# The last output tile of a hybrid encoder layer, computed in two runs of tokens

## The chip, the cores and the metric

The kernel runs on one core of a Trainium2 chip. A core has five engines with instruction queues of their own: TensorE (PE; PEld in a profile is its weight load), VectorE (DVE), ScalarE (ACT), GpSimd (POOL) and SyncE (SP, which only issues transfers here), beside 16 DMA engines. The metric is the device time of one execution in microseconds (us); less is better. The profile is of one execution, whose own time is given beside its span, the time from its first to its last instruction.

## The reference

One layer of a streaming encoder works on 256 prompt tokens and 32 sample tokens together, 288 in all, with a model width of 2048. A pooling mixer and a state-space mixer come first, then a gated feed-forward part, and each half ends with a normalised residual. Only the end matters here:

```python
up = hn @ p['w_up']
up, new_fconv = causal_dwconv(up, hist_fconv, p['ffn_conv_w'], p['ffn_conv_b'])
gate, val = up[..., :D_FF], up[..., D_FF:]
f = (jax.nn.silu(gate) * val) @ p['w_down']
x = x + rmsnorm(f, p['norm_ffn_post'])
```

`rmsnorm` divides each token's row of 2048 by the root of its mean square. So no output of a token is known before all 2048 columns of its `f` are: each of the 16 output tiles of `w_down` adds to the sum of squares. Everything is float32.

## The kernel before

**Layout.** Activations lie turned: 128 features in the partitions, 288 tokens along the free axis (`NT`). `BLK` names the three blocks of tokens: tokens 0 to 127 (first block), 128 to 255 (second block) and the 32 samples. A float32 product is made of three products in the type fp32r: weights and activations are each split into a high part (`hi`, made by ScalarE) and a low part (`lo`, the rest, made by VectorE). `mm3` (L162) issues them: high by high, high by low, low by high. Each of the three lines loads a 128x128 weight and streams 288 columns.

**`project`** (L167) fetches weights on SP's queue (`fetch_w`), splits them (`split_w`) and runs `mm3` over K tiles, for two output tiles of 128 features at a time. Hooks let other work be placed at a K group, and `done` is called with each finished accumulator. Accumulators come from a PSUM pool of five banks (`acc_ps`), other PSUM tiles from a pool of three (`aux_ps`).

**The down projection** runs in two halves of K, 22 tiles each. The first half's results lie in SBUF as `part`. The second half runs over `f2`, the last 22 activation tiles, in the loop at L1083: eight projections of two output tiles each. For each tile `down_out` (L1071) adds the accumulator to `part[t]`, squares it, and scales it by `g_ffn_post`. For tiles 0 to 13 the squares are summed over tiles in `fsum` on GpSimd; for tiles 14 and 15 `feature_sums` (L1059) sums them over features on TensorE, straight into `p_f`. That is a product with a column of ones: two over 128 tokens each and four over the 32 samples, whose result is wanted in four groups of partitions. `fsum` is summed the same way once, ahead of the last group of K tiles.

**Back to tokens.** The output has tokens in rows. Tiles 0 to 13 are turned through DRAM: VectorE transposes 32x32 blocks (`blocks_out`, L203), SP writes them to `fd` and reads them back as `ft` (a tile of 128 tokens by 512 features for each quarter q and block b; the fourth quarter's is `ft3`, 256 features wide) and `ft_s` for the samples. Tiles 14 and 15 are turned by TensorE into the PSUM tiles `last` (`to_tokens`, L1036). `xr` and `xr_s` hold the residual in the same layout.

**The end.** `token_rstd` (L588 on) makes the three columns of factors `rf` from `p_f` with one square root and one reciprocal. Then `y_out` (L1100) multiplies `ft` by the factor and adds it to `xr` on VectorE, and SP sends the result out, 256 KB at a time: three quarters of both blocks, then the samples (sent from ScalarE's queue, L1115), then the last quarter, in two instructions for each block because its halves lie in `ft3` and in `last`.

A scheduler places instructions in each engine's queue by priorities; `keep_in_program_order` pins an instruction to its place in the text. In the built program the last projection alternates its two output tiles after every K group, and the sums and turns of tiles 14 and 15 follow the last product.

Of the kernel before, what the change touches and what calls it, by code (L numbers as in the profile page):

```python
# [8 lines left out]
F32 = mybir.dt.float32  # L9
F32R = mybir.dt.float32r  # L10
AF = mybir.ActivationFunctionType
ALU = mybir.AluOpType
# [4 lines left out]
P = 128  # L17
TC = {"schedule_with_timeline_sim": True}
D_MODEL = 2048
NP_ = 256  # L20
NS = 32
NT = NP_ + NS
# [6 lines left out]
KD = D_MODEL // P  # L29
# [4 lines left out]
BLK = ((0, P), (P, P), (NP_, NS))  # L34
WINDOWS = (2, 4, 8, 16)
HALF = NF // 2
# [9 lines left out]
def body(  # L46
# [38 lines left out]
    act, dve, pool, pe, sp = nc.scalar, nc.vector, nc.gpsimd, nc.tensor, nc.sync  # L85
# [10 lines left out]
    const = ctx.enter_context(tc.tile_pool(name="const", bufs=1))  # L96
# [3 lines left out]
    acc_ps = ctx.enter_context(tc.tile_pool(name="acc_ps", bufs=5, space=PSUM))  # L100
# [3 lines left out]
    def aux(shape, name):  # L104
        return aux_ps.tile(shape, F32, tag="aux", name=name)
# [22 lines left out]
    def fetch_w(view, kb, nk, c0, nc_):  # L128
        raw = wpool.tile([P, nk, nc_], F32, tag="raw", name="raw")
        with tc.high_priority(offset=ahead[0]):  # L130
            sp.dma_start(out=raw, in_=view[:, kb : kb + nk, c0 : c0 + nc_])
        return raw

    def split_w(raw, kb, nk, nc_, after=()):

        out = []
        step = min(nk, 1024 // nc_)
        for k in range(0, nk, step):
            n = min(step, nk - k)
# [22 lines left out]
    def mm3(out, wh, wl, a, start, stop):  # L162
        pe.matmul(out, wh, a[:, 0, :], start=start, stop=False)  # L163
        pe.matmul(out, wh, a[:, 1, :], start=False, stop=False)  # L164
        pe.matmul(out, wl, a[:, 0, :], start=False, stop=stop)  # L165
# [82 lines left out]
    start = ExitStack()  # L248
# [20 lines left out]
    for i, v in enumerate((ssd_dt_bias, ssd_a_log, ssd_d)):  # L269
# [5 lines left out]
        out=pf_in[:, 4:6, :], in_=state_ffn_conv.rearrange("o b r (t p) -> t (o b r) p", p=P)  # L275
# [77 lines left out]
    p_ = aux([P, NT], "prs")  # L353
# [7 lines left out]
    pb, pah, g_mix_post, g_ffn_pre, g_ffn_post, pa, p_scale, g_ssd, pc, pf = prm  # L361
# [76 lines left out]
    r = htile("r", tag="z")  # L438
# [21 lines left out]
    for b, (o, go) in enumerate(((0, 0), (P, 256), (TAIL, MW - P))):  # L460
        p_ = aux([P, 3, HEADS], "ptok")
# [11 lines left out]
    p_ = aux([P, 2 * NX], "phv")  # L473
# [6 lines left out]
    for i in range(4):  # L480
        o = btile("bc")
# [5 lines left out]
    for gi in range(2):  # L487
        blocks_out(b_d, gi, bc[gi], mp)
        p_ = aux([P, MW], "pcb")
# [98 lines left out]
    def token_rstd(p_, scale, name):  # L588

        o = const.tile([P, 3], F32, tag="trs", bufs=2, name=name)  # L590
        act.activation(o, p_[:, 0:3], AF.Sqrt, bias=eps_t, scale=scale)
        dve.reciprocal(o, o)
        return o
# [228 lines left out]
    for gi in range(2):  # L822
        c = slice(gi * P, (gi + 1) * P)
# [76 lines left out]
    for s in range(KD + 2):  # L900
# [98 lines left out]
    part = []  # L999
# [34 lines left out]
    last = {}  # L1034

    def to_tokens(t):  # L1036

        if t < KD - 2:
            blocks_out(fd, t, part[t], fp)
            q, n = t // 4, (t % 4 + 1) * P  # L1040
            if t % 4 == 3 or t == KD - 3:
                c = slice(512 * q, 512 * q + n)
                for b in range(2):
                    sp.dma_start(out=ft[2 * q + b][:, :n], in_=fd[b * P : (b + 1) * P, c])
                sp.dma_start(out=ft_s[NS * q : NS * (q + 1), :n], in_=fd[NP_:NT, c])
            return
        j = t - KD + 2
        if j == 0:
            last.update({b: aux([P, 2 * P], "pft") if b == 2 else acc_ps.tile([P, 2 * P], F32, tag="acc", name="pft") for b in range(3)})
        for b, (o, n) in enumerate(BLK):  # L1050
            c = slice(j * P, (j + 1) * P)
            if b == 2:
                pe.matmul(last[b][P - NS :, c], part[t][:, o : o + n], ident, start=True, stop=True)
            else:
                pe.transpose(last[b][:, c], part[t][:, o : o + n], ident)
        if j == 1:
            act.activation(ft_s[P - NS :, 2 * P :], last[2][P - NS :, :], AF.Copy)

    def feature_sums(sq, first_, last_):  # L1059
        for b in range(2):  # L1060
            pe.matmul(
                p_f[:, b : b + 1], sq[:, b * P : (b + 1) * P], ones[:, 0:1],
                start=first_ and b == 0, stop=False, skip_group_check=True,
            )
        for q in range(4):
            pe.matmul(
                p_f[NS * q : NS * q + NS, 2:3], sq[:, NP_:], ones[:, 0:1],
                start=False, stop=last_ and q == 3, skip_group_check=True,
            )

    def down_out(t, p_):  # L1071
        dve.tensor_tensor(part[t], part[t], p_, op=ALU.add)
        if t < KD - 2:
            sq_add(fsum, part[t], fp, t == 0)
        else:
            q = fp.tile([P, NT], F32, tag="fr", bufs=2, name="fsq")
            with tc.high_priority(offset=400):
                act.activation(q, part[t], AF.Square)
            feature_sums(q, False, t == KD - 1)
        act.activation(part[t], part[t], AF.Copy, scale=g_ffn_post[:, t : t + 1])  # L1080

    n_tok = [0]
    for m in range(0, KD, 2):  # L1083
        def hook(kb, n):
            if m and kb == 16:
                while n_tok[0] < m:
                    to_tokens(n_tok[0])
                    n_tok[0] += 1
            if m == KD - 2 and kb == 16:
                feature_sums(fsum, True, False)  # L1090

        project(
            wdv[:, HALF:, :], [(m * P, 256)], f2, [(0, 8), (8, 8), (16, 6)], hook,
            lambda j, p_: down_out(m + j, p_),
        )
    to_tokens(KD - 2)
    to_tokens(KD - 1)
    rf = token_rstd(p_f, 1.0 / D_MODEL, "rf")

    def y_out(q, b):  # L1100

        x = xr[2 * q + b]
        f_ = ft[2 * q + b]
        for o, n, src in (
            ((0, 512, f_),) if q < 3 else ((0, 2 * P, f_[:, : 2 * P]), (2 * P, 2 * P, last[b]))
        ):
            c = slice(o, o + n)
            dve.scalar_tensor_tensor(x[:, c], src, rf[:, b : b + 1], x[:, c], op0=ALU.mult, op1=ALU.add)  # L1108
        sp.dma_start(out=y_prompt[0][b * P : (b + 1) * P, 512 * q : 512 * (q + 1)], in_=x)

    for q in range(3):
        y_out(q, 0)
        y_out(q, 1)
    dve.scalar_tensor_tensor(xr_s, ft_s, rf[:, 2:3], xr_s, op0=ALU.mult, op1=ALU.add)
    act.dma_start(out=y_sample[0].rearrange("s (q c) -> q s c", q=4), in_=xr_s)  # L1115
    y_out(3, 0)
    y_out(3, 1)
    ffn.close()


# [29 lines left out]
```

## Time and profile before

| | us |
|---|---|
| median of 3 runs | 1357.07 (1357.01 to 1357.39) |
| profiled execution | 1357.63 |
| its span | 1355.8 |
| PE busy | 1337.4 |
| DVE, ACT, POOL busy | 884.0, 667.0, 237.6 |
| granted TensorE clock, mean | 0.996 |

An engine's time is the sum over its instructions, in which overlapping ones count once. A row of the timeline gives start, duration, engine, line, operation and tile (result, then sources), shapes, and how often it stands there in a row. With "x4" the duration is from the first one's start to the last one's end. In brackets stands how long the engine had been idle and what ended that. A product of plain float32 data shows as two records of PE, one of fp32r data as one. The part of the trace that matters is the last 36 us: the projection of tiles 14 and 15 from about 1321, and what comes behind it.

### The profile page before, as it was taken

How to read it: one execution, taken by the hardware profiler on the slowest of the kernel's cores; microseconds unless marked ns; L12 is line 12 of the kernel's file. 1: busy time of each engine (PE TensorE's matmuls, PEld its weight loads, DVE VectorE, ACT ScalarE, POOL GpSimd, SP SyncE). 2: the span in 40 equal slices, each digit the busy share in tenths (PEclk: the TensorE clock that was granted, in tenths of full speed). 3: DMA queues.
4: the chain of work that ended last, by engine and by line, in shares of the span. 5: the costliest groups of instructions: out<-in, count | busy, mean ns of one | idle time of the engine just before them, and what ended most of it. 6: DMA issues, size and time to landing. Idle time of an engine off the chain costs nothing.

```text
span 1355.8 us, 25731 instructions
## 1 busy us (share of the span) xinstructions
PE 1337.4 (99%) x10201; PEld 1327.3 (98%) x10201; DVE 884.0 (65%) x1515; ACT 667.0 (49%) x997; POOL 237.6 (18%) x394
## 2 busy tenths in 40 slices
PE   8999999999999999999999999999999999999996
PEld 7999999999999999999999999999999999999995
DVE  6898988779644469977666643435666667654443
ACT  6557757446534455644444433334444444454441
POOL 3132112222224310311121100001112112101110
PEclk9999999999999999999999999999999999999998
DMA  8879885565756536866545555555545545576652
GB/s 268 249 190 277 257 245 172 156 220 153 241 180 209 170 111 202 244 180 193 171 158 173 160 155 159 169 179 163 179 156 165 177 156 167 168 226 201 189 163 88
DMA packets 300136, 252.13 MB, mean 186 GB/s; under 512 B 75729, under 2 KB 293051, under 8 KB 299887
## 3 DMA queue, kind: packets, MB, share of 16 engines
q1 hardware_dynamic: 296810, 243.20, 59.2%
q0 software_dynamic: 2320, 4.65, 1.2%
q10 hardware_dynamic: 884, 2.63, 0.5%
q8 instruction: 80, 1.31, 0.4%
q14 instruction: 42, 0.34, 0.1%
HBM read 236.13 MB, written 14.31 MB: 185 GB/s over the span
## 4 chain that ended last, share of the span: by engine, by line
PE 98%; DVE 0%; DMA 0%; SPq 0%; issue 0%; DVEq 0%; ACT 0%
PE acc L163 31%; PE acc L165 31%; PE acc L164 31%; PE pst L852 1%; PE py L562 1%; DMA xt<-in_x_prompt 0%; DVE xr L1108 0%; PE acc_x L164 0%; PE acc_x L165 0%; PE acc_x L163 0%; PE py L564 0%; PE pt L301 0%; PE acc L186 0%; PE pt L299 0%; PE acc L185 0%; PE py L568 0%
## 5 line engine op out<-in xcount | busy, mean ns | idle before, releaser
L147 DVE TENSOR_TENSOR wlo<-raw,whi 128x1024 fp32r<-128x1024 f32 (+1 forms) x416 | 493.8, 1189 | 350.7 <-ACT whi L146 340.2
L146 ACT ACTIVATE whi<-raw 128x1024 fp32r<-128x1024 f32 (+1 forms) x416 | 427.0, 1028 | 505.6 <-PE acc L164 429.5
L163 PE MATMUL acc<-hn,whi 128*128 128x288 f32 x1376 | 404.6, 295 | 0.0
L164 PE MATMUL acc<-hn,whi 128*128 128x288 f32 x1376 | 403.5, 294 | 0.0
L165 PE MATMUL acc<-hn,wlo 128*128 128x288 f32 x1376 | 403.2, 294 | 0.0
L164 PEld LDWEIGHTS acc<-hn,whi 128*128 128x128 f32 x1376 | 259.8, 189 | 0.1
L165 PEld LDWEIGHTS acc<-hn,wlo 128*128 128x128 f32 x1376 | 259.6, 189 | 0.0
L163 PEld LDWEIGHTS acc<-hn,whi 128*128 128x128 f32 x1376 | 257.3, 187 | 0.1
L163 PE MATMUL acc<-xn,whi 128*128 128x288 f32 x704 | 209.5, 299 | 0.0
L163 PE MATMUL acc<-fa,whi 128*128 128x288 f32 x704 | 208.6, 296 | 0.0
L164 PE MATMUL acc<-fa,whi 128*128 128x288 f32 x704 | 208.4, 296 | 0.0
L164 PE MATMUL acc<-xn,whi 128*128 128x288 f32 x704 | 208.2, 297 | 0.0
L165 PE MATMUL acc<-fa,wlo 128*128 128x288 f32 x704 | 208.0, 295 | 0.0
L165 PE MATMUL acc<-xn,wlo 128*128 128x288 f32 x704 | 207.5, 297 | 0.0
L164 PEld LDWEIGHTS acc<-xn,whi 128*128 128x128 f32 x704 | 133.8, 190 | 0.3
L165 PEld LDWEIGHTS acc<-xn,wlo 128*128 128x128 f32 x704 | 133.2, 190 | 0.3
L163 PEld LDWEIGHTS acc<-xn,whi 128*128 128x128 f32 x704 | 132.6, 189 | 0.5
L164 PEld LDWEIGHTS acc<-fa,whi 128*128 128x128 f32 x704 | 132.7, 188 | 0.0
L163 PEld LDWEIGHTS acc<-fa,whi 128*128 128x128 f32 x704 | 132.2, 188 | 0.0
L165 PEld LDWEIGHTS acc<-fa,wlo 128*128 128x128 f32 x704 | 132.0, 188 | 0.0
L944 POOL COPY fc_stage<-ebuf 128x4 f32<-128x4 f32 x88 | 27.9, 317 | 505.7 <-DVE ebuf L943 505.7
L950 DVE SCALAR_TENSOR_TENSOR fc<-ebuf,pf,fc 128x290 f32<-128x290 f32 x176 | 90.3, 517 | 2.8 <-ACT fc L948 0.2
(310 smaller groups left out, 1621.6 us busy)
## 6 DMA issues: line engine op xcount, KB each, us to landing
raw<-in_w_up SPq DMA_DIRECT2D x80, 1024.0 KB, 5.2
raw<-in_w_in SPq DMA_DIRECT2D x40, 1024.0 KB, 6.1
raw<-in_w_down SPq DMA_DIRECT2D x32, 1024.0 KB, 5.4
raw<-in_w_out SPq DMA_DIRECT2D x24, 1024.0 KB, 5.9
raw<-in_w_down SPq DMA_DIRECT2D x16, 768.0 KB, 4.6
raw<-in_w_up SPq DMA_DIRECT2D x14, 512.0 KB, 4.2
gb<-g_d SPq DMA_DIRECT2D x8, 832.0 KB, 5.0
raw<-in_w_in SPq DMA_DIRECT2D x6, 512.0 KB, 6.5
```

Of the source, the lines that this page charges most:

```text
L146: act.activation(hi, raw[:, k : k + n, :], AF.Copy)
L147: dve.tensor_tensor(lo, raw[:, k : k + n, :], hi.bitcast(F32), op=ALU.subtract)
L163: pe.matmul(out, wh, a[:, 0, :], start=start, stop=False)
L164: pe.matmul(out, wh, a[:, 1, :], start=False, stop=False)
L165: pe.matmul(out, wl, a[:, 0, :], start=False, stop=stop)
L562: ins = pe.matmul(y[c, 0:256], xw[:, 0, f_], m[:, h, 0:256], start=True, stop=False)
L852: ins = pe.matmul(st[:, o, :], x_, btok[:, gi, b, :], start=b != 1, stop=b != 0)
L944: pool.tensor_copy(fc_stage[:, :, :, i], e[:, 256:324].rearrange("p (s c) -> p s c", c=34)[:, :, 0:2])
L950: dve.scalar_tensor_tensor(c, e[:, r_ : r_ + 290], pf[:, r_, i : i + 1], c, op0=ALU.mult, op1=ALU.add)
```

## The change

- The loop over projections stops after tile 13. The weights of tiles 14 (`A`) and 15 (`B`) are still fetched together, but split one tile at a time, and tile 14 is computed alone, with `mm3` over all 288 tokens. Tiles 12 and 13 are sent to `fd` within it.
- Tile 15 is computed in two runs over its 22 K tiles: first the second block and the samples (`C1`, 160 tokens), then the first block (`C0`, 128 tokens). In `last_mm`, the high and low part of the activations are one moving operand for the high weights (two segments of columns, 320 or 256 in all), whose results lie side by side in one bank; the low weights' product (160 or 128 columns) goes to the first of them. The two are added on VectorE (`add_to`).
- The last K tile has three separate products into a small bank of its own (`p_c`), which is added as the third.
- The sums of `fsum`, now with tile 14's squares added to it, and the turn of tile 14 stand inside run 1. The sums for the second block and samples, their factors, and the turns of tile 15's second block and samples stand inside run 2, and so do these tokens' outputs, except the last quarter. The samples leave on SP's queue.
- `last` has 512 columns: ScalarE copies `ft3` into its first 256, so that the last quarter is one instruction for each block.
- Of the first block's four outputs, the first is made on TensorE: the identity times `xr[0]`, plus a diagonal of the factors (made on ScalarE) times `ft[0]`; ScalarE copies the sum to SBUF. The others stay on VectorE.
- Nearly all of this is pinned to program order.

```diff
-    def feature_sums(sq, first_, last_):
...
+    def first_sums(sq, first_):
+
+        pin(pe.matmul(p_f[:, 0:1], sq[:, :P], ones[:, 0:1], start=first_, stop=not first_, skip_group_check=True))
+
+    def other_sums(sq, first_):
+
+        pin(pe.matmul(p_f[:, 1:2], sq[:, P:NP_], ones[:, 0:1], start=False, stop=False, skip_group_check=True))
         for q in range(4):
-            pe.matmul(
+            pin(pe.matmul(
                 p_f[NS * q : NS * q + NS, 2:3], sq[:, NP_:], ones[:, 0:1],
...
+    def factors(c, name):
+        o = const.tile([P, 3], F32, tag="trs", bufs=2, name=name)[:, c]
+        pin(act.activation(o, p_f[:, c], AF.Sqrt, bias=eps_t, scale=1.0 / D_MODEL))
+        pin(dve.reciprocal(o, o))
+        return o
...
-    for m in range(0, KD, 2):
+    for m in range(0, KD - 2, 2):
...
-    to_tokens(KD - 2)
-    to_tokens(KD - 1)
-    rf = token_rstd(p_f, 1.0 / D_MODEL, "rf")
...
+    A, B = KD - 2, KD - 1
+    K22 = [(0, 8), (8, 8), (16, 6)]
+    raws = [fetch_w(wdv[:, HALF:, :], kb, n, A * P, 256) for kb, n in K22]
+
+    def one_tile(t):
+        out = []
+        for (kb, n), raw in zip(K22, raws):
+            out += split_w(raw[:, :, (t - A) * P : (t - A + 1) * P], kb, n, P)[0]
+        return out
+
+    p_a = acc_ps.tile([P, NT], F32, tag="acc", name="acc")
+    for k, hi, lo in one_tile(A):
+        if k == 8:
+            to_tokens(KD - 4)
+            to_tokens(KD - 3)
+        mm3(p_a, hi, lo, f2[k], k == 0, k == HALF - 1)
+    wb = one_tile(B)
+
+    last = [acc_ps.tile([P, 4 * P], F32, tag="acc", name="pft") for b in range(2)] + [aux([P, 2 * P], "pft")]
+
+    p_b = [acc_ps.tile([P, 2, n], F32, tag="acc", name="acc") for n in (NT - P, P)]
+    p_c = [aux([P, NT - P], "acc_c"), aux([P, P], "acc_c")]
+
+    def tile_out(t, c, p_, sq):
+        with tc.high_priority(offset=400):
+            dve.tensor_tensor(part[t][:, c], part[t][:, c], p_, op=ALU.add)
+            act.activation(sq[:, c], part[t][:, c], AF.Square)
+            act.activation(part[t][:, c], part[t][:, c], AF.Copy, scale=g_ffn_post[:, t : t + 1])
...
+    def last_mm(r, k, hi, lo, c):
+
+        if k == HALF - 1:
+            for i, (w, x) in enumerate(((hi, 0), (hi, 1), (lo, 0))):
+                pin(pe.matmul(p_c[r], w, f2[k][:, x, c], start=not i, stop=i == 2))
+            return
+        o, end = p_b[r], k == HALF - 2
+        pin(pe.matmul(o, hi, f2[k][:, :, c], start=k == 0, stop=end, skip_group_check=True))
+        pin(pe.matmul(o[:, 0, :], lo, f2[k][:, 0, c], start=False, stop=end, skip_group_check=True))
+
+    def add_to(t, c, p_):
+        return pin(dve.tensor_tensor(part[t][:, c], part[t][:, c], p_, op=ALU.add))
...
+    for k, hi, lo in wb:
+        last_mm(0, k, hi, lo, C1)
+        if k == 8:
+            first_sums(fsum, True)
+            other_sums(fsum, True)
+            for b in range(3):
+                turn(A, b)
+            for b in range(2):
+                act.activation(last[b][:, : 2 * P], ft[6 + b][:, : 2 * P], AF.Copy)
+    for x in range(2):
+        add_to(B, C1, p_b[0][:, x, :])
+    tile_out(B, C1, p_c[0], sq[B])
+    for k, hi, lo in wb:
+        last_mm(1, k, hi, lo, C0)
+        if k == 5:
+            other_sums(sq[B], False)
+            rf = factors(slice(1, 3), "rf1")
+        if k == 8:
+            turn(B, 1)
+            turn(B, 2)
+            act.activation(ft_s[P - NS :, 2 * P :], last[2][P - NS :, :], AF.Copy)
...
+    for q in range(3):
+        y_out(q, 1, rf[:, 0:1])
+    pin(dve.scalar_tensor_tensor(xr_s, ft_s, rf[:, 1:2], xr_s, op0=ALU.mult, op1=ALU.add))
+    pin(sp.dma_start(out=y_sample[0].rearrange("s (q c) -> q s c", q=4), in_=xr_s))
+    for x in range(2):
+        add_to(B, C0, p_b[1][:, x, :])
+    add_to(B, C0, p_c[1])
+    pin(act.activation(sq[B][:, C0], part[B][:, C0], AF.Square))
+    y_out(3, 1, rf[:, 0:1])
+    first_sums(sq[B], False)
+
+    p_y = acc_ps.tile([P, 512], F32, tag="acc", name="py_")
+    pin(pe.matmul(p_y, ident, xr[0], start=True, stop=False))
+    rf = factors(slice(0, 1), "rf0")
+    pin(act.activation(part[B][:, C0], part[B][:, C0], AF.Copy, scale=g_ffn_post[:, B : B + 1]))
+    turn(B, 0)
+    diag = fp.tile([P, P], F32, tag="fc", bufs=6, name="diag")
+    pin(act.activation(diag, ident, AF.Copy, scale=rf[:, 0:1]))
+    pin(pe.matmul(p_y, diag, ft[0], start=False, stop=True))
+    pin(act.activation(xr[0], p_y, AF.Copy))
+    y_out(1, 0, rf[:, 0:1])
+    y_out(2, 0, rf[:, 0:1])
+    pin(sp.dma_start(out=y_prompt[0][0:P, 0:512], in_=xr[0]))
+    y_out(3, 0, rf[:, 0:1])
```

Here L1127 and L1128 are the two products of `last_mm` in the changed kernel, L1124 its three products for the last K tile, and `turn` moves one block of a tile into `last` on TensorE.

More of the change, by code (lines that the diff above doesn't have):

```diff
@@ L1033, in body @@
     fd = dram.tile([NT, D_MODEL], F32, name="fd")
-    last = {}
+    pin = tc.keep_in_program_order
     def to_tokens(t):
[L1038 to L1057, printed above, removed]
@@ L1059, in feature_sums @@
-    def feature_sums(sq, first_, last_):
[L1060 to L1064, printed above, removed]
+        blocks_out(fd, t, part[t], fp)
+        q, n = t // 4, (t % 4 + 1) * P
+        if t % 4 == 3 or t == KD - 3:
+            c = slice(512 * q, 512 * q + n)
+            for b in range(2):
+                sp.dma_start(out=ft[2 * q + b][:, :n], in_=fd[b * P : (b + 1) * P, c])
+            sp.dma_start(out=ft_s[NS * q : NS * (q + 1), :n], in_=fd[NP_:NT, c])
@@ L1065, in feature_sums @@
+    def first_sums(sq, first_):
+        pin(pe.matmul(p_f[:, 0:1], sq[:, :P], ones[:, 0:1], start=first_, stop=not first_, skip_group_check=True))
+    def other_sums(sq, first_):
+        pin(pe.matmul(p_f[:, 1:2], sq[:, P:NP_], ones[:, 0:1], start=False, stop=False, skip_group_check=True))
         for q in range(4):
-            pe.matmul(
+            pin(pe.matmul(
                 p_f[NS * q : NS * q + NS, 2:3], sq[:, NP_:], ones[:, 0:1],
-                start=False, stop=last_ and q == 3, skip_group_check=True,
-            )
+                start=False, stop=not first_ and q == 3, skip_group_check=True,
+            ))
@@ L1071, in down_out @@
+    def factors(c, name):
[3 more added lines that the diff above has]
+        return o
     def down_out(t, p_):
         dve.tensor_tensor(part[t], part[t], p_, op=ALU.add)
[L1073 to L1079, printed above, removed]
+        sq_add(fsum, part[t], fp, t == 0)
@@ L1088, in hook @@
                     n_tok[0] += 1
-            if m == KD - 2 and kb == 16:
-                feature_sums(fsum, True, False)
         project(
@@ L1095, in body @@
         )
-    to_tokens(KD - 2)
-    to_tokens(KD - 1)
-    rf = token_rstd(p_f, 1.0 / D_MODEL, "rf")
-    def y_out(q, b):
-        x = xr[2 * q + b]
[L1103 to L1109, printed above, removed]
@@ L1111, in body @@
-    for q in range(3):
[L1112 to L1117, printed above, removed]
+    A, B = KD - 2, KD - 1
[6 more added lines that the diff above has]
+        return out
@@ new lines, in tile_out, with turn @@
+    def tile_out(t, c, p_, sq):
[3 more added lines that the diff above has]
+            act.activation(part[t][:, c], part[t][:, c], AF.Copy, scale=g_ffn_post[:, t : t + 1])
+    def turn(t, b):
+        c = slice((t - A) * P, (t - A + 1) * P)
+        if b == 2:
+            pin(pe.matmul(last[2][P - NS :, c], part[t][:, NP_:], ident, start=True, stop=True))
+        else:
+            pin(pe.transpose(last[b][:, 2 * P + c.start : 2 * P + c.stop], part[t][:, b * P : (b + 1) * P], ident))
@@ new lines, in body @@
+    sq = {t: fp.tile([P, NT], F32, tag="fr", bufs=2, name="fsq") for t in (A, B)}
+    tile_out(A, slice(0, NT), p_a, sq[A])
+    dve.tensor_tensor(fsum, fsum, sq[A], op=ALU.add)
+    C1, C0 = slice(P, NT), slice(0, P)
+    for k, hi, lo in wb:
[5 more added lines that the diff above has]
+                turn(A, b)
+            for b in range(2):
+                act.activation(last[b][:, : 2 * P], ft[6 + b][:, : 2 * P], AF.Copy)
@@ new lines, in body, with y_out @@
+    for x in range(2):
[10 more added lines that the diff above has]
+            act.activation(ft_s[P - NS :, 2 * P :], last[2][P - NS :, :], AF.Copy)
+    def y_out(q, b, rf):
+        x = xr[2 * q + b]
+        pin(dve.scalar_tensor_tensor(x, ft[2 * q + b] if q < 3 else last[b], rf, x, op0=ALU.mult, op1=ALU.add))
+        pin(sp.dma_start(out=y_prompt[0][b * P : (b + 1) * P, 512 * q : 512 * (q + 1)], in_=x))
```

## The prediction

> **What bounds the kernel now.** First the page: which engine carries the chain that ends last.
>
> ```profile
> PE 1337.4 (99%) x10201; PEld 1327.3 (98%) x10201; DVE 884.0 (65%) x1515; ACT 667.0 (49%) x997; POOL 237.6 (18%) x394
> PE 98%; DVE 0%; DMA 0%; SPq 0%; issue 0%; DVEq 0%; ACT 0%
> ```
>
> TensorE is the bound, and everything it does ahead of the last output tile is the same in both kernels. So two places count: TensorE's work from the start of the last two tiles, and what follows its last weight product. The second is read in the timeline (start, duration, engine, line).
>
> ```profile
> 1339.51 0.29 PE L165 MATMUL acc<-fa,wlo 128*128 128x288 f32 x1
> 1339.84 0.46 DVE L1072 TENSOR_TENSOR part<-part,acc 128x288 f32<-128x288 f32 x1 [0.34 <-PE acc L165]
> 1340.74 0.44 PE L1055 MATMUL pft<-ident,part 128*128 128x128 f32 x2
> 1341.44 0.60 PE L1061 MATMUL psum_f<-ones,fsq 128*128 128x1 f32 x4
> 1342.15 0.44 PE L1055 MATMUL pft<-ident,part 128*128 128x128 f32 x2
> 1342.29 0.26 ACT L591 ACTIVATE rf<-psum_f,eps_t 128x3 f32<-128x3 f32 x1 [0.84 <-PE psum_f L1066]
> 1342.59 0.18 DVE L592 RECIPROCAL rf<-rf 128x3 f32<-128x3 f32 x1 [2.29 <-ACT rf L591]
> 1342.80 4.07 DVE L1108 SCALAR_TENSOR_TENSOR xr<-ft,rf,xr 128x512 f32<-128x512 f32 x6
> 1347.56 1.15 ACTq L1115 DMA_DIRECT2D out<-xr_s  x1
> 1348.62 0.48 DVE L1108 SCALAR_TENSOR_TENSOR xr<-pft,rf,xr 128x256 f32<-128x256 f32 x1
> ```
>
> Consecutive weight products start 0.13 us apart, so the last slot ends at 1339.51 + 0.13 = 1339.65. Call that point E. Sums and turns take 3.1 us to the reciprocal; eleven VectorE instructions then run back to back to 1349.1, and none could begin earlier, because `rf` needs the last tile. The SP queue's waits and the windows show the rest (columns: stretch, its length, PE, PEld, DVE, ACT, POOL, granted clock, DMA share, GB/s).
>
> ```profile
> SPq L1146 <- DMA out<-xr: 5.0, 2, 4.4
> 1349.00:1350.00 1.00, 0.00 (x0) 0.00 (x0) 0.10 (x1) 0.00 (x0) 0.00 (x0) 0.50 0.72 115
> 1352.00:1353.00 1.00, 0.00 (x0) 0.00 (x0) 0.00 (x0) 0.00 (x0) 0.00 (x0) 0.50 0.25 86
> 1353.00:1354.00 1.00, 0.00 (x0) 0.00 (x0) 0.00 (x0) 0.00 (x0) 0.00 (x0) 0.50 0.23 86
> ```
>
> The last transfer is issued at 1349.13 (0.33 us); SP then waits 5.0 us, to 1354.5, and closing takes 1.3 us. Other output transfers land 2.2 us (median) after issue. The DMA share of a quarter at the end is 4 of 16 engines: the sample rows' transfer (L1115), issued late, holds back the last one's share there. So the tail is 16.15 us: 9.5 to the last issue, 5.4 to landing, 1.3 closing.
>
> **Price of one product.** Three rows of this kernel give the slots (first a window; then the timeline).
>
> ```profile
> 1240.00:1280.00 40.00, 40.00 (x303) 40.00 (x301) 18.99 (x23) 16.65 (x22) 4.56 (x4) 1.00 0.69 195
> 496.42 0.61 PE L852 MATMUL pst<-btok,xw_p 128*128 128x128 f32 x4
> 129.68 0.65 PE L562 MATMUL py<-m,xw 128*64 128x256 f32 x4
> 130.16 0.39 PE L564 MATMUL py<-m,xw 128*64 128x128 f32 x4
> ```
>
> - 288 columns of split (fp32r) data: 40/303, 0.133 us with missing records allowed for, or 0.462 ns per column. So 320 columns 0.148 and 256 columns 0.118.
> - Narrow: every fp32r product here has 288 columns, so 160 and 128 are not shown. L852, plain fp32 with a 128x128 weight, has single records of 0.275 us, so its slots are (0.61 - 0.275)/3 = 0.112 us for 128 columns. The one-column sums L1061 have the same spacing: a new 128-column weight sets it, not the columns. L564, with half the weight columns, is no slower per pass. I take 0.112 us for 160 and 128 columns. Below it lies pure streaming, 0.074 and 0.059. Above it lie the wide slot, 0.133, and plain fp32: two records per product, so 0.224 for 128 columns and 0.280 for 160.
>
> The Trainium skill ("TensorE: Matmul & The Clock Gate", Back-to-back issue gap) gives about 81 ns for a sustained pair of weight load and 128-column matmul; L852 shows 112, so the row is used. As an estimate from that page, 48 slots at 81 ns would take another 48 x 0.031 = 1.5 us off.
>
> **The change, part by part.**
>
> 1. *Tile order.* Tile 14 runs alone, then 15: 66 products each, at the same price. The first three splits need the weights up to twice as early, but the DMA share falls to 0.02 by 1320-1324, with all weights landed before the tiles start at 1321.4. The second use needs three further splits of 1.06 and 1.23 us each; they follow as tile 14 frees buffers (about 1324.6 and 1327.8), before tile 15's start at 1330.2. Cost 0; without that cover, one split pair, some 2.3 us.
> 2. *Two runs.* Tile 15 took 66 x 0.133 = 8.8 us. Run 1 (160 tokens): 21 x (0.148 + 0.112) + 3 x 0.112 = 5.80. Run 2 (128 tokens): 21 x (0.118 + 0.112) + 3 x 0.112 = 5.17. Sum 10.97: +2.2 us.
> 3. *Sums and turns inside the stream.* Before, the sums of `fsum` stood there once, 0.7 us (L165 at 1327.60, next product 1328.34, its successor 0.1 late). Now: all sums and tile 14's turn, 0.71 + 0.70 from the starts 1340.74, 1341.44, 1342.15; the other sums in run 2 without one 128-column sum (two slots), 0.49; tile 15's two turns, 0.53; plus about 0.1 at returns to products. Sum 2.5: +1.8. The run-2 sums wait for three adds (160 columns, about 0.33 each), and a square (0.34): ready 1.35 us after run 1, reached after 6 x 0.23 = 1.38. If late, TensorE waits that much.
>    E moves by 2.2 + 1.8 = +4.0, to 1343.65.
> 4. *Hidden under run 2.* The second block and the samples need only run 1: their reciprocal, three outputs (0.66 spacing) and the sample rows end some 5.2 us into a run 2 of 6.2 us. VectorE is free for the last adds, with 1 us to spare; were the sample rows late, those adds queue behind them. Their four transfers move from ACT's and SP's end to SP's front. ACT's two copies of `ft3` stand ahead of tile 15's square; their reads were issued at 1331.7, landed in 2.5, and run 1 ends at 1337.4: 3 us of cover.
> 5. *The new tail, from E.* Two adds from the first bank begin ahead of E; 288 columns take 0.46 and a column about 1.05 ns (L1108: 0.75 at 512, 0.48 at 256), so 128 take 0.29 and the third ends at 0.78. Square (0.45 less 0.13): 1.14. Two slots of sum and drain: 1.58. Square root 0.26, reciprocal 0.18, hand-offs 0.04: 2.11. ACT has to scale part of tile 15 first, then the diagonal: 2.62. The diagonal's product, 512 plain columns: L562 to L564 is 0.48 us for 256, so 0.9 and drain 0.17: 3.8. ACT's copy, 0.63 by the 128x512 split row: 4.48. SP issues it, and 0.39 us later the last block, whose own addition (three outputs of 0.75, overlapping) ended at 4.2: 4.87. Landing 2.2, closing 1.25: 8.3 us in place of 16.15.
>
> Sum: +4.0 - 7.85 = -3.9 us on the span of 1355.8, or 1351.9. The profiled execution took 1357.63, 1.8 us around its span, and is 0.56 above the median of the runs; -3.9 from 1357.07 gives **1353.2 us**. Its own range, 1352.0 to 1355.0, has a slot missed by 0.02 us (48 x 0.02 = 1.0) and a tail off by 1 us.
>
> **Rivals.**
>
> *Narrow products cost plain fp32 (slower).* Place: the 48 products of 160 or 128 columns, among them the whole last K tile. For it: none narrower than 288 runs in fp32r, and L562 shows 4-byte data that takes two records and 0.94 ns a column in each (0.48/2/256). Against: the fp32r records are single and take 0.46 ns a column. Price: 24 x (0.280 - 0.112) + 24 x (0.224 - 0.112) = 6.7, so 1359.9 us. It decides from 0.112 + 3.9/48 = 0.19 us a narrow slot. The Trainium skill ("FP8 and Floating Point Precision", TensorE Precision Notes) counts four passes for true FP32 and a truncating read for the reduced form, without a width. No run so far shows a narrow one.
>
> *Narrow slots cost the wide slot, 0.133.* For it: L185, 64 weight columns, keeps the 0.133 spacing, so a cost per fp32r product may be fixed. Against: L852. Price 48 x 0.021 + 21 x 0.015 = 1.3: 1354.5.
>
> *Narrow products stream.* Weight loads hide wholly: 24 x 0.038 + 24 x 0.053 = 2.2 less: 1351.0. L852 speaks against it.
>
> *The change doesn't shorten the tail.* If the four-engine transfer still ended last, six to seven us after an issue 1.1 us ahead of E, it would add about 1 us: inside the first range, and no case of its own.
>
> **How the numbers follow.** Forecast 0.50, plain fp32 0.28, wide slot 0.14, streaming 0.08. A measurement of this kernel tells 0.2% (2.7 us) from no change: faster is below 1354.4, slower above 1359.8. Faster: 0.93 of the forecast, half of the wide slot, all streaming: 0.61. Slower: over half of plain fp32, 0.16. Within: 0.23. The range runs from streaming's 1351.0 to just over the slow rival's middle, 1360.0; with the halves beyond both ends it leaves out under 2 in 10.
>
> **What would show it.** Right: L1127/L1128 pairs start about 0.26 us apart in run 1 and 0.23 in run 2; E near 1343.6; SP's last issue 4.9 us behind E, landing in about 2.2; no DMA share of a quarter at the end. Wrong: pairs at 0.37 to 0.43 us (plain fp32); TensorE waiting for ACT at the run-2 sums, or for splits in tile 14; VectorE still on the sample rows at E; or a last landing later than 3 us.

## The result

| | before | changed |
|---|---|---|
| median of 21 runs each | 1357.03 (1356.21 to 1358.31) | 1355.12 (1354.13 to 1356.92) |
| ratio, with 95% interval | | 0.9986 (0.998 to 0.9992) |
| profiled execution | 1357.63 | 1354.13 |
| its span | 1355.8 | 1352.2 |
| first product of tiles 14 and 15 | 1321.34 | 1320.12 |
| start of the last weight product, from there | 18.18 | 22.51 |
| from that start to the end of the span | 16.33 | 9.61 |
| both together | 34.50 | 32.12 |

The changed kernel is 1.9 us faster, 0.14%. That is a real gain (the interval stays below 1), but half of the 3.9 us that was forecast, and inside the 0.2% that was set as the bound of "no change". The two spans differ by 3.6 us, of which 1.2 lie ahead of the change: tiles 14 and 15 begin 1.2 us earlier, though TensorE's instructions up to there are the same. Their first product, before and, in a fence of its own, changed:

```profile
1321.34 0.29 PE L163 MATMUL acc<-fa,whi 128*128 128x288 f32 x1
```

```profile
1320.12 0.29 PE L163 MATMUL acc<-fa,whi 128*128 128x288 f32 x1
```

That is scatter: executions with the same instructions up to there began those tiles at 1320.1 and at 1322.9. So traces are compared below from the first product of tiles 14 and 15 on ("the last part"). By that measure the change took off 2.4 us: +4.3 in TensorE's work, -6.7 behind it.

The page of the changed kernel gives the same first answer as before: TensorE is the bound, and it has slightly more to do.

```profile
PE 1340.3 (99%) x10217; PEld 1328.7 (98%) x10217; DVE 883.2 (65%) x1519; ACT 668.8 (49%) x1004; POOL 237.7 (18%) x394
PE 99%; DMA 0%; DVE 0%; ACT 0%; issue 0%; DVEq 0%
```

The timeline of the changed kernel, in the last part (start, duration, engine, line, tiles, shapes):

```profile
1328.78 0.30 PE L165 MATMUL acc<-fa,wlo 128*128 128x288 f32 x1
...
1329.14 0.35 PE L1127 MATMUL acc<-fa,whi 128*128 128x320 f32 x1
1329.32 0.24 PE L1128 MATMUL acc<-fa,wlo 128*128 128x160 f32 x1
1329.40 0.35 PE L1127 MATMUL acc<-fa,whi 128*128 128x320 f32 x1
...
1335.91 0.68 DVE L1131 TENSOR_TENSOR part<-part,acc 128x160 f32<-128x160 f32 x2 [5.30 <-PE acc L1128]
1335.93 0.28 PE L1124 MATMUL acc_c<-fa,wlo 128*128 128x160 f32 x1
...
1336.26 0.33 PE L1127 MATMUL acc<-fa,whi 128*128 128x256 f32 x1
1336.43 0.22 PE L1128 MATMUL acc<-fa,wlo 128*128 128x128 f32 x1
1336.49 0.33 PE L1127 MATMUL acc<-fa,whi 128*128 128x256 f32 x1
...
1337.06 0.32 DVE L1109 TENSOR_TENSOR part<-part,acc_c 128x160 f32<-128x160 f32 x1 [0.47 <-DVE part L1131]
1337.42 0.34 ACT L1110 ACTIVATE fsq<-part 128x160 f32<-128x160 f32 x1 [3.85 <-DVE part L1109]
1337.80 0.38 PE L1053 MATMUL psum_f<-ones,fsq 128*128 128x1 f32 x2 [0.23 <-ACT fsq L1110]
...
1341.69 0.65 SPq L1168 DMA_DIRECT2D out<-xr_s  x1
...
1342.63 0.28 PE L1124 MATMUL acc_c<-fa,wlo 128*128 128x128 f32 x1
...
1346.53 0.60 ACT L1184 ACTIVATE xr<-py__15574 128x512 f32<-128x512 f32 x1 [1.22 <-PE py__15574 L1183]
1347.16 0.33 SPq L1187 DMA_DIRECT2D out<-xr  x1
1347.58 0.41 SPq L1163 DMA_DIRECT2D out<-xr  x1
```

To be seen: a pair of products takes 0.26 us in run 1 (1329.14 to 1329.40) and 0.23 in run 2 (1336.26 to 1336.49). In run 1 the third add (L1109) begins 0.47 us after the second has ended, though the products that it adds ended at 1336.21, and the sums of run 2 (L1053) wait for the square that follows it. The last weight product starts at 1342.63, so the last slot ends at E = 1342.74; the last transfer is issued 4.84 us later. SP's waits, and the transfers of the last 13 us (tile, queue, count, KB each, median us from issue to landing):

```profile
SPq L1217 <- DMA out<-xr: 2.9, 2, 2.3
```

```profile
q1 hardware_dynamic: 1284, 2.36, 49.1%
...
out<-xr SPq DMA_DIRECT2D x8, 256.0 KB, 3.4
out<-xr_s SPq DMA_DIRECT2D x1, 256.0 KB
```

In the kernel before, a prompt transfer landed in 2.2 us. Here the median is 3.4, and the last lands 3.4 us after its issue. (The median of before hides its last two, which took 5.6 and 5.4.) The tail is 4.8 to the last issue, 3.4 to landing and 1.3 closing.

### The profile page after: what moved, and what is told of

It reads as the page before. It is cut to its first block, busy times and chain, and to the rows that moved or that the text cites. A ratio compares the mean times of both kernels' runs of the same rounds, so it can differ in the third digit from the quotient of the medians.

```text
span 1352.2 us, 25779 instructions
## 1 busy us (share of the span) xinstructions
PE 1340.3 (99%) x10217; PEld 1328.7 (98%) x10217; DVE 883.2 (65%) x1519; ACT 668.8 (49%) x1004; POOL 237.7 (18%) x394
## 4 chain that ended last, share of the span: by engine, by line
PE 99%; DMA 0%; DVE 0%; ACT 0%; issue 0%; DVEq 0%
PE acc L163 31%; PE acc L165 31%; PE acc L164 31%; PE pst L852 1%; PE py L562 1%; PE acc L1127 1%; PE acc_x L164 0%; PE acc_x L165 0%; PE acc_x L163 0%; PE py L564 0%; DMA xt<-in_x_prompt 0%; PE pt L299 0%; PE pt L301 0%; PE acc L1128 0%; PE acc L186 0%; PE pt L300 0%
## 5 line engine op out<-in xcount | busy, mean ns | idle before, releaser
L163 PE MATMUL acc<-fa,whi 128*128 128x288 f32 x682 | 201.9, 296 | 0.0
L164 PE MATMUL acc<-fa,whi 128*128 128x288 f32 x682 | 201.9, 296 | 0.0
L165 PE MATMUL acc<-fa,wlo 128*128 128x288 f32 x682 | 201.5, 295 | 0.0
L164 PEld LDWEIGHTS acc<-fa,whi 128*128 128x128 f32 x682 | 128.6, 188 | 0.0
L163 PEld LDWEIGHTS acc<-fa,whi 128*128 128x128 f32 x682 | 128.1, 188 | 0.0
L165 PEld LDWEIGHTS acc<-fa,wlo 128*128 128x128 f32 x682 | 127.9, 188 | 0.0
L939 POOL COPY ebuf<-pf 128x2 f32<-128x2 f32 x88 | 74.4, 846 | 126.2 <-DVE fc L950 52.4
```

Source lines behind the costliest of these rows:

```text
L939: pool.tensor_copy(e[:, 258:260], pf[:, 4:6, i])
```

## The experiments

Eleven kernels were run. "Last part" is the time from the first product of tiles 14 and 15 to the end of the span in one profiled execution; there, stretches with equal instructions agree within about 0.1 us. Single executions of one kernel scatter by 2 us and more, so a cause is read from the last part, and the ratio says what it is worth. Ratios are to the kernel before, run on the same chip.

| run | median | ratio (95%) | last part |
|---|---|---|---|
| before | 1357.03 | 1 | 34.50 |
| the change | 1355.12 | 0.9986 (0.998 to 0.9992) | 32.12 |
| samples in four transfers | 1353.45 | 0.9974 (0.9964 to 0.9985) | 30.85 |
| samples on ScalarE's queue | 1354.68 | 0.9983 (0.9974 to 0.9992) | 32.15 |
| column sums later | 1354.71 | 0.9982 (0.9973 to 0.9992) | 32.20 |
| no bank of its own | 1354.33 | 0.9982 (0.9973 to 0.9991) | 31.63 |
| no diagonal | 1354.74 | 0.9984 (0.9975 to 0.9993) | 32.16 |
| three narrow products | 1357.2 | 1.0001 (0.9992 to 1.0011) | 34.43 |
| one run of tokens | 1356.96 | 0.9999 (0.999 to 1.0009) | 34.37 |
| four transfers, sums later | 1352.66 | 0.9971 (0.996 to 0.9982) | 30.42 |
| four transfers, no own bank | 1353.17 | 0.9972 (0.9961 to 0.9984) | 30.19 |
| four transfers, no own bank, sums later | 1352.84 | 0.9969 (0.9956 to 0.9981) | 30.16 |
| before, samples in four transfers | 1354.37 | 0.9982 (0.9973 to 0.9991) | 31.92 |

### The sample rows' transfer

The sample rows leave in one transfer whose pattern has the four quarters as its slowest dimension. The trace has a mark for each part of a transfer that lands. In the changed kernel (us from the span's start; ordinary numbers of the trace, not a view):

```
sample rows (issued 1341.69):            1342.76 | 1347.16 1347.40 1347.64 1347.75
second block, quarter 3 (issued 1344.30): 1346.99 ... 1347.54 (12 marks), 1347.82 1348.11 1348.27 1348.38
last transfer (issued 1347.58):           1349.86 ... 1350.20 (12 marks), 1350.38 1350.63 1350.85 1350.96
```

Four parts carry the samples and come 5.5 to 6.1 us after the issue. A prompt transfer has 16 marks, and of each that follows, four come last. The Trainium skill ("DMA: Bandwidth & Descriptors", Why a DMA increments its semaphore by 16 and not by 1) says that a transfer uses as many engines as the largest number up to 16 that divides the slowest dimension of both its sides, and that the unused ones' share of the count is written at once. The trace agrees: one early mark and four late ones for a slowest dimension of 4.

*Four transfers.* The samples in four transfers of 32 rows each, on the same queue:

```diff
-    pin(sp.dma_start(out=y_sample[0].rearrange("s (q c) -> q s c", q=4), in_=xr_s))
+    for q in range(4):
+        pin(sp.dma_start(out=y_sample[0][:, 512 * q : 512 * (q + 1)], in_=xr_s[NS * q : NS * (q + 1), :]))
```

> The sample rows go out in four transfers of 32 rows each instead of one whose outer dimension is 4. Theory (the one transfer runs on 4 engines for about 6 us and holds back its neighbours there and the transfers queued behind it): from SP's last issue to the end of its waits 3.4 us becomes 2.6 to 2.8, the second block's last quarter lands about 2.2 us after its issue in place of 4.1, the end comes 0.7 us earlier from TensorE's last product, and the time is about 0.7 us under that of the changed kernel (ratio to before about 0.998). Rival (the four transfers of the first block, 0.69 us of all engines each, issued within 1.9 us, are bound by the rate alone): the 3.4 us stay, within 0.2.

The transfers of its last 12 us, and SP's waits:

```profile
q1 hardware_dynamic: 1344, 2.36, 52.1%
...
out<-xr SPq DMA_DIRECT2D x8, 256.0 KB, 2.1
out<-xr_s SPq DMA_DIRECT2D x4, 64.0 KB, 1.7
```

```profile
SPq L1218 <- DMA out<-xr: 1.6, 3, 0.8
```

The same bytes, in 60 packets more (4 transfers with 16 marks each in place of one with 4). A sample transfer now lands in 1.7 us, the prompt's in 2.1, the last one in 2.3 in place of 3.4. The last issue is where it was (18.8 us after tile 14's last product, in both), and the last part is 1.27 us shorter, more than the 0.7 expected: 1.09 in landing, and closing takes 1.1 in place of 1.3. The bytes are the same, and the prompt's transfers, 256 KB each as well, land in about 2 us with their 16 parts. So neither the bytes nor the size of the transfer held up the end, but its four parts. (The samples as one transfer in 16 parts were not tried.)

*The other queue.* The same single transfer, issued on ScalarE's queue (`act.dma_start`), as in the kernel before.

> The sample rows' one transfer goes out on ScalarE's queue, not SP's; nothing else is changed. If the four engines that it uses hold back the others' share there, it takes as long as on SP: last landing and tail (9.6 us) stay within 0.2. If it holds back what is queued behind it on SP's queue, the second block's last quarter lands about 2.2 us after its issue in place of 4.1, and the tail is 8.5 us or less, though four engines still carry the samples.

The samples take 6.07 us again, the second block's quarter 3 4.1, the last transfer 3.4. So a queue of its own does not help: the transfers meet behind the queues. Of each later one, four parts are the last again, which points to the four engines of the samples.

In this run the packets of the samples can be told from the others by their queue. Each of the four parts has 32 packets of 2 KB. The first starts at 1345.80. The first 16 of all take until 1347.7, up to 0.99 us each, though no other output is on its way between 1345.9 and 1347.1; from then on a packet takes 0.084 us as a rule. At that rate 32 in a row are 2.7 us. So, as an estimate, the small number of engines accounts for some 2.7 of the 6.07 us; the slow start is a cost of its own, which no run here explains.

*The kernel before, with four sample transfers.* Only this edit, on ScalarE's queue as there:

```diff
-    act.dma_start(out=y_sample[0].rearrange("s (q c) -> q s c", q=4), in_=xr_s)
+    for q in range(4):
+        act.dma_start(out=y_sample[0][:, 512 * q : 512 * (q + 1)], in_=xr_s[NS * q : NS * (q + 1), :])
```

> The kernel before with only its sample rows' transfer cut in four. Theory (the transfer over four engines holds up the end of any tail that it lies in, that of the kernel before as well): last landing from 5.4 us after the last issue down to 2 to 3, so 2.4 to 3.4 us shorter, ratio 0.9975 to 0.9985, as fast as the whole change or faster. Rival (three more issues on the queue and the amount to be moved make up for it): within 0.5 us of before, ratio 0.9996 to 1.0004.

SP's last waits in that kernel, and its transfers:

```profile
SPq L1147 <- DMA out<-xr: 2.0, 2, 1.3
SPq L1147 <- DMA out<-xr_s: 0.3, 1, 0.3
```

```profile
q10 hardware_dynamic: 192, 0.26, 11.8%
...
out<-xr_s ACTq DMA_DIRECT2D x4, 64.0 KB, 1.9
```

The samples' queue has 192 packets, 128 rows and 64 marks. SP's 5.0 us at the end become 2.0, and 0.3 for a sample transfer; the last transfer lands 3.0 us after its issue in place of 5.4, with the issue where it was (9.6 us after the start of the last product). The last part is 2.58 us shorter. One edit to one line is worth as much as the whole change (0.9982 against 0.9986, intervals that overlap). With the edit in both, the change itself is worth 1.07 us in the last part (30.85 against 31.92); the medians cannot tell that (0.9974 against 0.9982, intervals that overlap).

### Two runs, and what a narrow product costs

*One run.* Tile 15 in one run of three 288-column products for each K tile; all the rest behind it, as far as it can be kept (no bank of its own, and all outputs on VectorE, without the diagonal):

```diff
     for k, hi, lo in wb:
-        last_mm(0, k, hi, lo, C1)
+        mm3(p_b, hi, lo, f2[k], k == 0, k == HALF - 1)
...
-    for k, hi, lo in wb:
-        last_mm(1, k, hi, lo, C0)
```

> Tile 15 in one run over all 288 tokens with three products a K tile, its sums and turns after it, and all ten outputs after these, made by VectorE; tile 14 alone, the sums of fsum and the wide last quarter as in the changed kernel. Theory (splitting in two runs pays): TensorE's last product comes 3.6 us earlier than in the changed kernel, and the tail behind it is 16.15 us less one output instruction pair, so about 15.5 to 16 us in place of 9.5: slower than the changed kernel by 2 to 3 us, close to before. Rival (the order of outputs and the merged last quarter do it, not the split): the tail is under 13.5 us, and the time is within 0.5 us of the changed kernel or below it.

The last product starts at 1339.84, with 15.5 us behind it: the time of the kernel before again (34.37 against 34.50). VectorE's last output and SP's last five issues:

```profile
1346.04 5.16 SPq L1145 DMA_DIRECT2D out<-xr  x5
1347.87 0.75 DVE L1144 SCALAR_TENSOR_TENSOR xr<-pft,rf,xr 128x512 f32<-128x512 f32 x1
```

As it stands, the other edits bring nothing without the second run. But the sample rows' transfer is in this number too. It stands on SP's queue ahead of five outputs and is out from 1345.33 to 1350.84, and in that time two of SP's issues take 1.83 and 1.30 us in place of 0.33. So the last output, ready at 1348.62, is issued only at 1350.63 and lands 3.4 us later. From the first product of tile 14, VectorE ends after 27.65 us here, after 27.77 in the kernel before and after 26.88 in the changed one. As an estimate, with an issue at once, a landing of 2.3 to 3.0 and a closing of 1.1, as in the kernels with four sample transfers, the last part would be 31.1 to 31.8, against 30.85 for the change with four transfers. So two runs in place of one are worth 2.25 us beside the slow transfer (34.37 against 32.12), but by this estimate 0.2 to 0.9 without it. One run of tokens with four sample transfers was not tried.

*Three narrow products.* The high and low activations as two products in place of one operand:

```diff
-        pin(pe.matmul(o, hi, f2[k][:, :, c], start=k == 0, stop=end, skip_group_check=True))
+        for x in range(2):
+            pin(pe.matmul(o[:, x, :], hi, f2[k][:, x, c], start=k == 0 and x == 0, stop=end, skip_group_check=True))
```

> The high and low part of the activations go in two products instead of one moving operand. Theory (a product of 160 or 128 columns takes a slot of 0.112 us that its weight load sets): a K tile takes 0.336 us in both runs in place of 0.259 and 0.231, TensorE's last product comes 21 x (0.077 + 0.105) = 3.8 us later, and the kernel is slower than before by about 2 us (ratio 1.0014). Rival (the slot goes by columns, 0.46 ns each): a K tile takes 0.222 and 0.177 us, and the kernel is as fast as the changed one or faster.

The timeline of run 1 and of run 2 in this kernel:

```profile
1330.42 0.39 PE L1128 MATMUL acc<-fa,whi 128*128 128x160 f32 x2
1330.64 0.28 PE L1129 MATMUL acc<-fa,wlo 128*128 128x160 f32 x1
1330.75 0.39 PE L1128 MATMUL acc<-fa,whi 128*128 128x160 f32 x2
...
1339.19 0.38 PE L1128 MATMUL acc<-fa,whi 128*128 128x128 f32 x2
1339.35 0.19 PEld L1129 LDWEIGHTS acc<-fa,wlo 128*128 128x128 f32 x1
1339.41 0.28 PE L1129 MATMUL acc<-fa,wlo 128*128 128x128 f32 x1
...
1339.52 0.39 PE L1128 MATMUL acc<-fa,whi 128*128 128x128 f32 x2
```

Three products take 0.33 us whether they have 160 or 128 columns: 0.11 each, the number that the prediction took from L852. The Trainium skill ("TensorE: Matmul & The Clock Gate", LDWEIGHTS) gives the duration of a weight load as its columns divided by 1.2, in ns; as an estimate from it, 128 columns take 107. The trace's slot is near that, though a weight load itself is recorded with 0.19 us there and overlaps the next. The 81 ns that the Trainium skill gives under Back-to-back issue gap on the same page are not seen here: the slots are 0.11. The last product starts 3.4 us later, so the common operand pays for the double run. The end came only 2.3 us later, and the kernel is as fast as before (1.0001) where 1.0014 was expected: in the longer run 2 TensorE does not wait, and the sample rows' transfer is issued earlier ahead of the last one, which lands in 2.3.

### The bank of its own, and the late sums

*No bank of its own.* The last K tile like the others, and two adds in place of three:

```diff
-        if k == HALF - 1:
-            for i, (w, x) in enumerate(((hi, 0), (hi, 1), (lo, 0))):
-                pin(pe.matmul(p_c[r], w, f2[k][:, x, c], start=not i, stop=i == 2))
-            return
-        o, end = p_b[r], k == HALF - 2
+        o, end = p_b[r], k == HALF - 1
...
-    for x in range(2):
-        add_to(B, C1, p_b[0][:, x, :])
-    tile_out(B, C1, p_c[0], sq[B])
+    add_to(B, C1, p_b[0][:, 0, :])
+    tile_out(B, C1, p_b[0][:, 1, :], sq[B])
...
-    add_to(B, C0, p_c[1])
```

> The last K tile goes into the big bank like the others, with one moving operand; two adds in place of three. Theory (the own bank costs more than it hides): run 1 is 0.08 us shorter and run 2 0.10, the two adds begin 0.19 us after the last product and end 0.80 us after it where three now end 0.87 after it; the third add of run 1, which begins 0.4 us late, is gone, and with it TensorE's wait in run 2. End 0.5 to 0.7 us earlier than the changed kernel. Rival (the own bank pays by hiding two adds): the square begins 0.2 us or more later than now, counted from tile 14's last product, and the end with it.

The handover from run 1 to run 2 in this kernel:

```profile
1336.61 0.32 DVE L1126 TENSOR_TENSOR part<-part,acc 128x160 f32<-128x160 f32 x1 [5.55 <-PE acc L1123]
1336.97 0.32 DVE L1108 TENSOR_TENSOR part<-part,acc 128x160 f32<-128x160 f32 x1
...
1337.32 0.34 ACT L1109 ACTIVATE fsq<-part 128x160 f32<-128x160 f32 x1 [2.75 <-DVE part L1108]
...
1337.78 0.33 PE L1053 MATMUL psum_f<-ones,fsq 128*128 128x1 f32 x2
```

Two adds back to back, and L1053 waits for nothing. The bank was to let two adds begin before the last products; it costs three slots in place of a pair (0.336 against 0.26 and 0.23, 0.18 over both runs), the wait of 0.4, and at the end one more add (the square follows the last product's start by 0.90 us without it, by 1.01 with it). The last square and the last issue come 0.68 us earlier without the bank, the end 0.49: the samples' transfer, by then closer to the end, keeps the rest (the last landing takes 3.6 us in place of 3.4).

*Sums later.* The sums of run 2 behind K tile 7 (not 5), its turns behind 10 (not 8).

> The sums in run 2 stand behind K tile 7 instead of 5, and tile 15's turns behind K tile 10 instead of 8. Theory (the sums stand about 0.4 us too early, because VectorE's third add of run 1 begins 0.4 us late): TensorE doesn't wait there, run 2 takes 6.3 us in place of 6.7, and the last product and the end come 0.4 us earlier. Rival (the wait follows the sums wherever they are, because the third add waits for TensorE): run 2 stays at 6.7 us. In both, the sample rows are 0.46 us later and still done when the last adds begin.

The same sums as in the last view, in this kernel:

```profile
1338.65 0.32 DVE L1109 TENSOR_TENSOR part<-part,acc_c 128x160 f32<-128x160 f32 x1 [0.47 <-DVE part L1131]
...
1339.47 0.33 PE L1053 MATMUL psum_f<-ones,fsq 128*128 128x1 f32 x2
```

The late add stands there, but TensorE waits for nothing: run 2 takes 6.26 us in place of 6.70, and the last square comes 0.44 us earlier. The end does not come earlier: the samples are issued 12.9 us after tile 14's last product in both kernels, so here they stand 0.4 us closer to the last transfers. SP's last two issues take 0.60 us each in place of 0.33 and 0.41, so the last issue is only 0.16 us earlier, and its landing takes 3.6 us.

*Both.* Sums later and four sample transfers.

> The sample rows in four transfers and the sums of run 2 two K tiles later. Theory (two independent costs): run 2 takes 6.3 us as in the run with later sums, the tail from the last product 8.3 us as in the run with four transfers, so the end is 0.4 us earlier than with four transfers alone: ratio to before about 0.997. Rival (the sums' delay only moves the wait, since the sample rows are then later): the tail grows by 0.4 us, and the time is that of four transfers alone.

Here the 0.43 us reach the end (30.42 against 30.85): the two costs are independent, and that of the transfer had hidden that of the wait.

*Four transfers and no bank of its own; and the sums later as well.*

> The sample rows in four transfers and the last K tile in the common bank. Theory (two independent costs: the first saves 1.28 us behind the last square, the second 0.68 us ahead of it, which the slow transfer hid when the own bank was taken away alone): from tile 14's last product to the end about 21.5 us against 23.46 in the changed kernel, ratio to before 0.996 to 0.997. Rival (the time won ahead of the square is given back whatever the transfers do): no shorter than with four transfers alone, 22.2 us and 0.9974.

> Four transfers, the common bank, and the column sums later as well. Theory (the common bank has already taken away the wait of TensorE that the later sums take away): within 0.2 us of the run without the later sums. Rival (two waits, each with its own 0.4 us): another 0.4 us shorter.

Without the bank the 0.66 us reach the end too (30.19 against 30.85; from tile 14's last product 21.52, expected 21.5). Moving the sums in addition changes 0.03: the wait is gone already. By the last part these two are the shortest of all, 2 us shorter than the change and 4.3 shorter than before. The medians of all versions of the change with four transfers lie between 1352.66 and 1353.45, and their intervals overlap.

### The diagonal

All four quarters of the first block on VectorE, without the identity, the diagonal and ScalarE's copy:

```diff
-    pin(pe.matmul(p_y, ident, xr[0], start=True, stop=False))
...
-    pin(pe.matmul(p_y, diag, ft[0], start=False, stop=True))
-    pin(act.activation(xr[0], p_y, AF.Copy))
-    y_out(1, 0, rf[:, 0:1])
-    y_out(2, 0, rf[:, 0:1])
-    pin(sp.dma_start(out=y_prompt[0][0:P, 0:512], in_=xr[0]))
-    y_out(3, 0, rf[:, 0:1])
+    for q in range(4):
+        y_out(q, 0, rf[:, 0:1])
```

> The first block's first output is made by VectorE like the other three; no diagonal, no two products into a PSUM tile, no copy by ScalarE. Theory (the last transfers, not the making of the outputs, end the kernel): the fourth VectorE output ends within 0.1 us of where SP now issues the last transfer, 4.9 us behind TensorE's last product, and the end moves by less than 0.3 us. Rival (the product on TensorE takes 0.66 us off VectorE's chain): the end comes 0.5 us later or more.

VectorE's last output in this kernel's timeline, and in a fence of its own the same one in the changed kernel's:

```profile
1346.74 0.74 DVE L1162 SCALAR_TENSOR_TENSOR xr<-pft,rf,xr 128x512 f32<-128x512 f32 x1
```

```profile
1346.25 0.74 DVE L1162 SCALAR_TENSOR_TENSOR xr<-pft,rf,xr 128x512 f32<-128x512 f32 x1
```

Counted from tile 14's last product, VectorE ends 0.67 us later without the diagonal, one output. But the last issue is only 0.11 us later, because with the diagonal it stands on SP's queue behind ScalarE's copy (1346.53 to 1347.13, then L1187), and VectorE's result lies ready from 1346.99. The landing gives 0.08 of it back, so the end comes 0.03 us later. The diagonal is as long as what it replaces, but for 0.11 us at the last issue; with four sample transfers it was not tried.

## Why the prediction was half right

- **Narrow slots: right.** A pair of 0.260 and 0.230 was forecast; 0.259 and 0.230 stand in the trace. The slower rival (plain float32, 0.37 to 0.43 for a pair) and both others fall: the run with three products puts a slot at 0.11 for 160 and for 128 columns. By the time alone, the rival of the wide slot (1354.5) would have fitted better than the forecast.
- **Tile order, sums and turns in the stream: right.** No wait stands in tile 14, and no extra turn costs more than its slots.
- **E: +4.3 in place of +4.0.** The step that was off is the one on the run-2 sums: "ready 1.35 us after run 1, reached after 6 x 0.23 = 1.38". The square ended about 1.7 us after run 1, because VectorE's third add began 0.47 us late. TensorE waited the difference, as the text said it would if the square were late. With the sums later, or one add fewer, the 0.4 us are gone, and with the sums later alone E moves by 3.9.
- **The last issue: right.** 4.87 us behind E were forecast, 4.84 measured. So the order of adds, square, sum, root, diagonal and copies is as it was worked out. That the diagonal saves nothing in it was not seen: the forecast named its path and VectorE's (4.48 and 4.2 us behind E) and did not ask what the end would be without it.
- **The landing: the step that failed.** "Landing 2.2" was the median of the trace before; it is 3.4. The prediction saw the four-engine transfer hold back the last one in the kernel before, and dismissed it as a rival in which that transfer "still ended last". It did not end last (1347.75, against 1350.96 for the end), and it cost 1.3 us all the same, by putting the later transfers behind. The cost was named there as about 1 us, but as part of a range, not as a term of the sum. Of what the prediction set down as signs of being wrong, two came: TensorE waited at the run-2 sums, and the last landing took more than 3 us.

Together: 0.3 in E and 1.2 in the tail, 1.5 of the 1.9 us between the forecast of 1353.2 and the median of 1355.1. The rest is what the last part (-2.4) and the medians (-1.9) differ by, within the scatter of runs. The time lies in the range, though 0.1 us outside the forecast's own 1352.0 to 1355.0, and on the other side of the 0.2% from where most of the chance was put: the version with four sample transfers is the one that meets the forecast (1353.45).

What stays open: why the third add of run 1 starts 0.47 us late. By the trace its two sources were ready (at 1336.21 and 1336.59, for a start at 1337.06), it does so in every kernel that has it (0.47 in the runs with sums later, too), and the same add at the end of run 2 follows the second within 0.1 us. Also open is why even the other twelve parts of a later transfer come late: 1346.99 at the earliest for the second block's quarter 3, 2.7 us after its issue, against 1.9 with four sample transfers. The same goes for the slow start of the samples' own packets, and for SP's long issues while their transfer is out.

## What to carry to other kernels

Read how many parts each of the last transfers has, not only which of them lands last: here one with few parts delayed all that were issued after it, and a one-line edit of it was worth as much as a rewrite of the last tile. A gain ahead of such a transfer can disappear until it is mended (all of 0.44 us here, and 0.2 of 0.68), and another can look larger than it is (by the estimate above, the second run), so edits are to be measured again with the transfer mended. An edit that shortens one of two equal paths (the diagonal), or starts work early at the price of more steps (the bank of its own), has to be priced against the kernel without it.

## What the runs showed of the hardware

A 256 KB transfer in four parts took 5.5 to 6.1 us, four transfers of 64 KB in 16 parts 1.7 to 1.9 us each; which queue issued it changed nothing (6.06 and 6.07). On ScalarE's queue, the first 16 of its 128 packets took 1.9 us, with no other output under way for 1.2 of them, and the others 0.084 us each as a rule. While it was out, an issue on SP took up to 1.83 us in place of 0.33. A product with a new 128-column weight took 0.11 us at 128 and at 160 columns in fp32r; a pair takes what the 288-column rate gives for the wide one (0.148 or 0.118) plus 0.11. VectorE's add that begins 0.47 us late is in the trace of every kernel that has it and is unexplained.
